# A decoder trunk on one core: the down projections take the high and the low part of an activation chunk in one product of 512 columns

## The chip, the core and the metric

The kernel runs on one core of a Trainium2 chip. The core has a matrix engine (TensorE, "PE", whose weight loads the profile lists apart as "PEld"), a vector engine (VectorE, "DVE"), a scalar engine (ScalarE, "ACT"), a general engine (GpSimd, "POOL") and a queue that issues transfers (SyncE, "SP"). Each works through its own list of instructions in order and waits on semaphores for the others. Matrix products read both operands from SBUF and add into PSUM, which has eight banks of 512 f32 columns on 128 partitions. The metric is the device time of one execution in microseconds.

## The reference, cut to what matters

The trunk has two layers on 256 tokens of width 1024. Each layer is a feed-forward block, a token mixer, and another feed-forward block, so four feed-forward blocks in all. The change touches only the last product of `swiglu`, the down projection:

```
D_MODEL = 1024
SEQ = 256
DEPTH = 2
D_FF = 256 * ((8 * D_MODEL // 3 + 255) // 256)      # 2816
...
def swiglu(x, w_in, w_out):
    gate, up = jnp.split(x @ w_in, 2, axis=-1)
    return (jax.nn.silu(gate) * up) @ w_out
...
    for i in range(DEPTH):
        x = x + 0.5 * swiglu(rms_norm(x, ffn1_norm_g[i]), ffn1_w_in[i], ffn1_w_out[i])
        hn = rms_norm(x, mix_norm_g[i])
        ...
        x = x + jnp.concatenate([y_tok, y_mem], axis=-1) @ w_out
        x = x + 0.5 * swiglu(rms_norm(x, ffn2_norm_g[i]), ffn2_w_in[i], ffn2_w_out[i])
```

## The kernel before

Activations are kept transposed: features on the 128 partitions, the 256 tokens along the columns (T = 256). To keep f32 accuracy with the faster f32r products, every operand is split into a high part (the value rounded to f32r) and a low part (the remainder). A product of a weight chunk w and an activation chunk x is then three products that add into the same 256 columns: `mm3` (L224 to L228) issues wh times xh (L225), wh times xl (L226) and wl times xh (L227). The weight chunk, 128x128, is the operand that is loaded; the activation chunk, 128x256, is streamed. Each of the three has its own load, also where the first two load the same wh.

Weights come in tiles of four chunks by 256 columns: `wtile` (L216) issues a transfer of 512 KB on SP into one of five raw buffers, ACT rounds it to wh (L211), DVE subtracts to get wl (L212), each into one of eight buffers.

A feed-forward block (`ffn`, L509) first runs `ffn_in` (L471): eleven groups, each of two banks, with gate and up halves of 256 columns; `hidden` (L473) evacuates a group: two DVE products with the norm's row (L476), a Silu on ACT, two DVE products (L479), then the split into hi and lo units of 128x512 (`split_plain`, L244 to L246: L245 a cast on ACT, L246 a subtraction on DVE). A unit of 128x512 holds two chunks of 256 tokens side by side, so hi and lo of a pair of chunks are two tiles. The 11 pairs make 22 chunks.

Then the down projection: for each pair of output blocks c2 (four of them, 256 output features each), six weight tiles are taken in turn (`KG`: five of four chunks, one of two), and for each tile both output blocks m = 0, 1 get their chunks from `products`. Both blocks lie in one bank, m = 0 in columns 0 to 255 and m = 1 in 256 to 511. When all 22 chunks are in, DVE multiplies the bank by half the norm's row (L544) and adds the residual (L546); `Norm.put` then splits the result for the next stage with the gain (ACT L132, DVE L241), squares it (ACT) and adds up the squares (DVE L288), and folds the two halves after the fourth pair (L291). The next norm's sum over features is a product with a column of ones (`chain`, line 231 of the helper `mmf`), issued by PE some 7.5 us of planned time after the block ends; between lie products of the next stage, which need the parts xh and xl but not the norm. The last pair of the last block is apart: it takes the whole weight row at once and runs m = 0 to its end before m = 1.

The order on PE and SP is the order of the program, woven by `Weave`, which counts planned PE time in `wv.now` (`mm3` counts 0.328 us). The order on ACT and DVE is chosen by the scheduler of the language.

Of the kernel before, what the change touches and what calls it, by code (L numbers as in the profile page):

```python
# [11 lines left out]
F32R = mybir.dt.float32r  # L12
# [3 lines left out]
ALU = mybir.AluOpType  # L16
# [4 lines left out]
T = 256  # L21
# [77 lines left out]
def tile_trunk(ctx: ExitStack, tc: tile.TileContext, a, out):  # L99
    nc = tc.nc  # L100
    seq = [0]

    def mk(pool, shape, dt, tag):
        seq[0] += 1
        return pool.tile(shape, dt, tag=tag, name=f"{tag}_{seq[0]}")
# [5 lines left out]
    wv = Weave()  # L111
# [16 lines left out]
    tt = nc.vector.tensor_tensor  # L128
    tabled = [None]

    def act(*args, **kw):
        ins = nc.scalar.activation(*args, **kw)  # L132
        if args[2] not in (AF.Copy, AF.Square):
            tabled[0] = ins
# [6 lines left out]
    def unit(dt):  # L141
        return mk(up, [P, 2, T], dt, "u")

    def tmp():
        return mk(tp, [P, 2, T], F32, "t")
# [4 lines left out]
    def mo():  # L150
        return mk(pb8, [P, 512], F32, "bank")

    def halves(ps):
        return ps.rearrange("p (h t) -> p h t", h=2)
# [61 lines left out]
    def wtile(src, nk, ncol=256):  # L216
        raw = mk(wrp, [P, nk, ncol], F32, "wr")
        nc.sync.dma_start(raw, src)
        return split(raw, [P, nk, ncol])

    def wcols(w, c0, kh):
        return wtile(w.rearrange("(k p) f -> p k f", p=P)[:, kh * 4:(kh + 1) * 4, c0:c0 + 256], 4)

    def mm3(ps, wh, wl, xh, xl, start, stop):  # L224
        nc.tensor.matmul(ps, wh, xh, start=start, stop=False, skip_group_check=True)  # L225
        nc.tensor.matmul(ps, wh, xl, start=False, stop=False, skip_group_check=True)  # L226
        nc.tensor.matmul(ps, wl, xh, start=False, stop=stop, skip_group_check=True)  # L227
        wv.now += 0.328  # L228
# [15 lines left out]
    def split_plain(src, hi, lo):  # L244
        nc.scalar.copy(hi, src)  # L245
        tt(out=lo, in0=src, in1=hi.bitcast(F32), op=ALU.subtract)  # L246
# [10 lines left out]
    def pair(x):  # L257
        return x.unsqueeze(1).to_broadcast([P, 2, T])
# [209 lines left out]

    KG = [(0, 4), (4, 4), (8, 4), (12, 4), (16, 4), (20, 2)]

    def ffn_in(x, w_in, hh, hl, mid=None):  # L471

        def hidden(ps):  # L473
            t = tmp()
            for m in range(2):
                tt(out=t[:, m], in0=ps[m][:, :T], in1=x.rb, op=ALU.mult)  # L476
            act(t, t, AF.Silu)
            for m in range(2):
                tt(out=t[:, m], in0=t[:, m], in1=ps[m][:, T:], op=ALU.mult)  # L479
            hi, lo = unit(F32R), unit(F32R)  # L480
            split_plain(t, hi, lo)
            hh.append(hi)
            hl.append(lo)

        waiting = []
        for gi in range(11):
            ps = [mo(), mo()]
            for kh in range(2):
                for part in range(2):
                    wh, wl = wcols(w_in, part * FF + gi * 256, kh)  # L490
                    for m in range(2):
                        for k in range(4):
                            kc = kh * 4 + k
                            mm3(ps[m][:, part * T:(part + 1) * T],
                                wh[:, k, m * P:(m + 1) * P], wl[:, k, m * P:(m + 1) * P],
                                x.xh[kc // 2][:, kc % 2], x.xl[kc // 2][:, kc % 2],
                                start=kc == 0 and part == 0, stop=kc == 7)
                        yield
            waiting.append(ps)
            if gi == 0 and not x.done:  # L500
                continue
            yield x.ready
            for ps in waiting:
                hidden(ps)
            waiting.clear()
            if mid is not None and gi == 5:
                wv.spawn(mid())

    def ffn(x, w_in, w_out, nxt=None, mid=None):  # L509

        pieces[0] = 1
        hh, hl = [], []
        yield from ffn_in(x, w_in, hh, hl, mid)
        w = w_out.rearrange("(k p) f -> p k f", p=P)

        def products(ps, m, kg, wt, start):
            ms = slice(m * P, (m + 1) * P)
            for k in range(kg[1]):
                kc = kg[0] + k
                mm3(ps, wt[0][:, k, ms], wt[1][:, k, ms], hh[kc // 2][:, kc % 2], hl[kc // 2][:, kc % 2],  # L520
                    start=kc == 0 and start, stop=kc == 21)

        for c2 in range(4):
            wts = [(kg, w[:, kg[0]:kg[0] + kg[1], c2 * 256:(c2 + 1) * 256]) for kg in KG]
            if nxt is None and c2 == 3:
                wts = [(kg, wtile(src, kg[1])) for kg, src in wts]
                y = tmp()
                for m in range(2):
                    ps = mo()[:, :T]
                    for kg, wt in wts:  # L530
                        products(ps, m, kg, wt, True)
                        yield
                    tt(out=y[:, m], in0=ps, in1=x.hrb, op=ALU.mult)
                    tt(out=y[:, m], in0=y[:, m], in1=x.xT[c2][:, m], op=ALU.add)
                    nc.scalar.dma_start(out[:, 2 * c2 + m], y[:, m])
                return
            ps = mo()
            for kg, src in wts:
                wt = wtile(src, kg[1])
                for m in range(2):  # L540
                    products(ps[:, m * T:(m + 1) * T], m, kg, wt, m == 0)
                    yield
            t = tmp()
            tt(out=t, in0=halves(ps), in1=pair(x.hrb), op=ALU.mult)  # L544
            xn = unit(F32)
            tt(out=xn, in0=t, in1=x.xT[c2], op=ALU.add)  # L546
            if nxt is None:
                nc.scalar.dma_start(out[:, 2 * c2:2 * c2 + 2], xn)
            else:
                nxt.put(xn)  # L550
        wv.spawn(nxt.chain(), LAT['norm'])
# [424 lines left out]
    def program():  # L976
        yield from memory()
        x1, x2, x3 = Norm(G_MIX, half=False), Norm(G_F2), Norm(G_F1 + 8)
        x4, x5 = Norm(G_MIX + 8, rows=False), Norm(G_F2 + 8)
        yield from ffn(x0, a["ffn1_w_in"][0], a["ffn1_w_out"][0], x1, late_constants)  # L980
        yield from mixer_a(x1, x2)
        yield from ffn(x2, a["ffn2_w_in"][0], a["ffn2_w_out"][0], x3)
        yield from ffn(x3, a["ffn1_w_in"][1], a["ffn1_w_out"][1], x4, rope_tables)
        yield from mixer_b(x4, x5)
        yield from ffn(x5, a["ffn2_w_in"][1], a["ffn2_w_out"][1])
# [41 lines left out]
```

## Time and profile before

| | |
|---|---|
| median of 3 runs | 1012.15 us (1011.66 to 1013.83) |
| the profiled execution's own time | 1012.23 us |
| its span, first to last instruction | 1010.4 us |
| granted TensorE clock, mean over the span | 1.00 |
| PE, PEld, DVE, ACT busy | 998.5, 980.2, 655.5, 519.5 us |

The profile is taken by the hardware on one execution. Its views used below are the page (busy time, the chain of work that ended last, groups of instructions by line), the timeline (start and duration of instructions, us), the chain by time, and windows (busy time of PE, PEld, DVE, ACT and POOL in a stretch, with the number of instructions, the granted clock, the share of transfers and GB/s). Products overlap in PE's pipeline, so a product's duration is longer than the distance from one start to the next; that distance is called the pitch here. In a row such as "bank<-u,wh 128*128 128x256 f32 x896" the loaded operand's shape comes first, then the streamed one's, and the count. f32r operands are printed as f32.

### The profile page before, as it was taken

The numbers are of one execution on the slowest core, as the hardware profiler recorded it, in microseconds if no ns is written. First come the engines' busy times: TensorE is split into PE (matmuls) and PEld (weight loads), VectorE is DVE, ScalarE is ACT, GpSimd is POOL, SyncE is SP. The second block draws the span as 40 slices with busy tenths as digits, with TensorE's granted clock in tenths as the row PEclk, the third lists the DMA queues.
The fourth block names the chain that finished last, engine by engine and source line by source line (L and its number), as shares of the span: only waits on it lengthen the run. The fifth ranks groups of instructions, "written<-read, shape, count | busy, mean of one in ns | idle before, by whom it ended". The sixth has DMA issues, their size and how long they took to land.

```text
span 1010.4 us, 20624 instructions
## 1 busy us (share of the span) xinstructions
PE 998.5 (99%) x8594; PEld 980.2 (97%) x8594; DVE 655.5 (65%) x1063; ACT 519.5 (51%) x764; POOL 35.7 (4%) x32
## 2 busy tenths in 40 slices
PE   8999999999999999999999999999999999999998
PEld 7999999999999999999999999999987899999998
DVE  6866665577856676665558666656787766666551
ACT  7754445446656554444445544544557754454440
POOL 1200000000001000000000000000121000000000
PEclk9999999999999999999999999999999999999999
DMA  9776656666644566665676666567541347666550
GB/s 308 242 245 200 192 180 185 199 183 179 184 139 133 167 210 195 200 189 170 192 206 205 189 191 201 173 197 198 182 131 66 100 131 220 198 189 185 188 170 21
DMA packets 173204, 182.70 MB, mean 181 GB/s; under 512 B 7124, under 2 KB 168328, under 8 KB 173112
## 3 DMA queue, kind: packets, MB, share of 16 engines
q1 hardware_dynamic: 171872, 179.60, 58.3%
q10 hardware_dynamic: 1016, 1.58, 0.5%
q8 instruction: 67, 1.10, 0.5%
q0 software_dynamic: 224, 0.22, 0.2%
q14 instruction: 25, 0.20, 0.1%
HBM read 180.32 MB, written 1.05 MB: 180 GB/s over the span
## 4 chain that ended last, share of the span: by engine, by line
PE 94%; DVE 3%; ACT 1%; DMA 1%; POOL 0%; issue 0%; SPq 0%; ACTq 0%
PE bank L225 30%; PE bank L226 30%; PE bank L227 30%; PE bank L231 2%; PE bank L236 1%; ACT u L132 1%; DVE wl L212 1%; DMA wr<-in_mem_w_kv_dram 1%; PE bank L961 1%; POOL col L379 0%; DVE col L930 0%; DVE u L383 0%; DVE col L591 0%; PE bank L925 0%; DVE u L946 0%
## 5 line engine op out<-in xcount | busy, mean ns | idle before, releaser
L212 DVE TENSOR_TENSOR wl<-wr,wh 128x1024 fp32r<-128x1024 f32 (+1 forms) x347 | 414.7, 1196 | 279.8 <-ACT wh L211 279.0
L211 ACT CAST wh<-wr 128x1024 fp32r<-128x1024 f32 (+1 forms) x347 | 356.8, 1031 | 393.1 <-PE bank L226 368.9
L225 PE MATMUL bank<-xh,wh 128*128 128x256 f32 x1544 | 429.1, 278 | 0.0
L226 PE MATMUL bank<-xl,wh 128*128 128x256 f32 x1544 | 426.8, 276 | 0.0
L227 PE MATMUL bank<-xh,wl 128*128 128x256 f32 x1544 | 426.8, 276 | 0.0
L226 PEld LDWEIGHTS bank<-xl,wh 128*128 128x128 f32 x1544 | 290.3, 188 | 0.1
L225 PEld LDWEIGHTS bank<-xh,wh 128*128 128x128 f32 x1544 | 290.0, 188 | 0.1
L227 PEld LDWEIGHTS bank<-xh,wl 128*128 128x128 f32 x1544 | 289.9, 188 | 0.0
L225 PE MATMUL bank<-u,wh 128*128 128x256 f32 x896 | 249.3, 278 | 0.0
L226 PE MATMUL bank<-u,wh 128*128 128x256 f32 x896 | 247.6, 276 | 0.0
L227 PE MATMUL bank<-u,wl 128*128 128x256 f32 x896 | 247.6, 276 | 0.0
L225 PEld LDWEIGHTS bank<-u,wh 128*128 128x128 f32 x896 | 168.2, 188 | 1.9 <-issue 1.7
L226 PEld LDWEIGHTS bank<-u,wh 128*128 128x128 f32 x896 | 168.4, 188 | 0.1
L227 PEld LDWEIGHTS bank<-u,wl 128*128 128x128 f32 x896 | 168.3, 188 | 0.0
L225 PE MATMUL bank<-wh,xh 128*128 128x256 f32 x208 | 59.7, 287 | 0.0
L226 PE MATMUL bank<-wl,xh 128*128 128x256 f32 x208 | 57.9, 278 | 0.0
L227 PE MATMUL bank<-wh,xl 128*128 128x256 f32 x208 | 57.9, 278 | 0.0
L476 DVE TENSOR_TENSOR t<-bank,rb 128x256 f32<-128x256 f32 x88 | 36.6, 420 | 7.3 <-PE bank L227 7.3
L225 PEld LDWEIGHTS bank<-wh,xh 128*128 128x128 f32 x208 | 39.1, 188 | 0.5 <-issue 0.3
L226 PEld LDWEIGHTS bank<-wl,xh 128*128 128x128 f32 x208 | 39.1, 188 | 0.1
L227 PEld LDWEIGHTS bank<-wh,xl 128*128 128x128 f32 x208 | 39.0, 187 | 0.0
L479 DVE TENSOR_TENSOR t<-t,bank 128x256 f32<-128x256 f32 x88 | 32.7, 412 | 1.8 <-ACT t L132 1.8
(171 smaller groups left out, 657.5 us busy)
## 6 DMA issues: line engine op xcount, KB each, us to landing
wr<-in_ffn_w_in_dram SPq DMA_DIRECT2D x176, 512.0 KB, 3.6
wr<-in_ffn_w_out_dram SPq DMA_DIRECT2D x80, 512.0 KB, 3.5
wr<-in_a_w_in_dram SPq DMA_DIRECT2D x28, 512.0 KB, 3.9
wr<-in_b_w_in_dram SPq DMA_DIRECT2D x14, 512.0 KB, 4.6
wr<-in_a_w_out_dram SPq DMA_DIRECT2D x12, 512.0 KB, 3.3
wr<-in_b_w_out_dram SPq DMA_DIRECT2D x12, 512.0 KB, 3.4
wr<-in_ffn_w_out_dram SPq DMA_DIRECT2D x16, 256.0 KB, 2.8
wr<-in_mem_w_kv_dram SPq DMA_DIRECT2D x7, 512.0 KB, 8.0
```

The source lines that it names most:

```text
L132: ins = nc.scalar.activation(*args, **kw)
L211: last[0] = nc.scalar.copy(hi[:, i * n:(i + 1) * n], src[:, i * n:(i + 1) * n])
L212: tt(out=lo[:, i * n:(i + 1) * n], in0=src[:, i * n:(i + 1) * n], in1=hi[:, i * n:(i + 1) * n].bitcast(F32), op=ALU.subtract)
L225: nc.tensor.matmul(ps, wh, xh, start=start, stop=False, skip_group_check=True)
L226: nc.tensor.matmul(ps, wh, xl, start=False, stop=False, skip_group_check=True)
L227: nc.tensor.matmul(ps, wl, xh, start=False, stop=stop, skip_group_check=True)
L231: nc.tensor.matmul(ps, lhsT, rhs, start=start, stop=stop, skip_group_check=True)
L236: nc.tensor.transpose(ps, src, ident[:k, :k])
L476: tt(out=t[:, m], in0=ps[m][:, :T], in1=x.rb, op=ALU.mult)
L479: tt(out=t[:, m], in0=t[:, m], in1=ps[m][:, T:], op=ALU.mult)
L961: nc.tensor.matmul(o[es[e], cs], vr[:, i, js], pTs[e][:, src], start=i == 0, stop=i == 1, skip_group_check=True)
```

## The change

Each hidden chunk gets a unit of its own with its high part in columns 0 to 255 and its low part in columns 256 to 511. In the pairs on the wide path, one product of wh takes both parts, 512 columns into a bank of its own per output block; then wl times the high part adds into the first 256 columns of it. The second half of the bank holds wh times the low part, so before the multiplication by half the norm's row ACT copies that half to SBUF and DVE adds it to the first half, for each of the two blocks. Each output pair takes two banks instead of one. The last pair of the last feed-forward block keeps the three products. In `hidden`, the split is done per chunk, 256 columns at a time.

```
--- before.py
+++ after.py
@@ -468,7 +468,7 @@
 
     KG = [(0, 4), (4, 4), (8, 4), (12, 4), (16, 4), (20, 2)]
 
-    def ffn_in(x, w_in, hh, hl, mid=None):
+    def ffn_in(x, w_in, hid, mid=None):
 
         def hidden(ps):
             t = tmp()
@@ -477,10 +477,10 @@
             act(t, t, AF.Silu)
             for m in range(2):
                 tt(out=t[:, m], in0=t[:, m], in1=ps[m][:, T:], op=ALU.mult)
-            hi, lo = unit(F32R), unit(F32R)
-            split_plain(t, hi, lo)
-            hh.append(hi)
-            hl.append(lo)
+            for m in range(2):
+                u = unit(F32R)
+                split_plain(t[:, m], u[:, 0], u[:, 1])
+                hid.append(u)
 
         waiting = []
         for gi in range(11):
@@ -509,16 +509,23 @@
     def ffn(x, w_in, w_out, nxt=None, mid=None):
 
         pieces[0] = 1
-        hh, hl = [], []
-        yield from ffn_in(x, w_in, hh, hl, mid)
+        hid = []
+        yield from ffn_in(x, w_in, hid, mid)
         w = w_out.rearrange("(k p) f -> p k f", p=P)
 
-        def products(ps, m, kg, wt, start):
+        def products(ps, m, kg, wt, wide):
+
             ms = slice(m * P, (m + 1) * P)
             for k in range(kg[1]):
                 kc = kg[0] + k
-                mm3(ps, wt[0][:, k, ms], wt[1][:, k, ms], hh[kc // 2][:, kc % 2], hl[kc // 2][:, kc % 2],
-                    start=kc == 0 and start, stop=kc == 21)
+                if wide:
+                    u = hid[kc].rearrange("p a b -> p (a b)")
+                    nc.tensor.matmul(ps, wt[0][:, k, ms], u, start=kc == 0, stop=False, skip_group_check=True)
+                    nc.tensor.matmul(ps[:, :T], wt[1][:, k, ms], u[:, :T], start=False, stop=kc == 21,
+                                     skip_group_check=True)
+                    wv.now += 0.328
+                else:
+                    mm3(ps, wt[0][:, k, ms], wt[1][:, k, ms], hid[kc][:, 0], hid[kc][:, 1], kc == 0, kc == 21)
 
         for c2 in range(4):
             wts = [(kg, w[:, kg[0]:kg[0] + kg[1], c2 * 256:(c2 + 1) * 256]) for kg in KG]
@@ -528,20 +535,23 @@
                 for m in range(2):
                     ps = mo()[:, :T]
                     for kg, wt in wts:
-                        products(ps, m, kg, wt, True)
+                        products(ps, m, kg, wt, False)
                         yield
                     tt(out=y[:, m], in0=ps, in1=x.hrb, op=ALU.mult)
                     tt(out=y[:, m], in0=y[:, m], in1=x.xT[c2][:, m], op=ALU.add)
                     nc.scalar.dma_start(out[:, 2 * c2 + m], y[:, m])
                 return
-            ps = mo()
+            ps = [mo(), mo()]
             for kg, src in wts:
                 wt = wtile(src, kg[1])
                 for m in range(2):
-                    products(ps[:, m * T:(m + 1) * T], m, kg, wt, m == 0)
+                    products(ps[m], m, kg, wt, True)
                     yield
-            t = tmp()
-            tt(out=t, in0=halves(ps), in1=pair(x.hrb), op=ALU.mult)
+            t, low = tmp(), tmp()
+            for m in range(2):
+                nc.scalar.copy(low[:, m], ps[m][:, T:])
+                tt(out=t[:, m], in0=ps[m][:, :T], in1=low[:, m], op=ALU.add)
+            tt(out=t, in0=t, in1=pair(x.hrb), op=ALU.mult)
             xn = unit(F32)
             tt(out=xn, in0=t, in1=x.xT[c2], op=ALU.add)
             if nxt is None:
```

## The prediction

> **What bounds the kernel now.** I read the page's head and its chain first, then the waits of TensorE, then stretches of the four down projections.
>
> ```profile
> span 1010.4 us, 20624 instructions
> PE 998.5 (99%) x8594; PEld 980.2 (97%) x8594; DVE 655.5 (65%) x1063; ACT 519.5 (51%) x764; POOL 35.7 (4%) x32
> PE 94%; DVE 3%; ACT 1%; DMA 1%; POOL 0%; issue 0%; SPq 0%; ACTq 0%
> ```
>
> TensorE (PE) carries 94% of the chain that ended last, and its weight loads (PEld) are nearly as busy as its products. That it is busy does not say what limits one product, so I looked at a down projection instruction by instruction. The first two fences below are the timeline at the start and at the end of the first one (start us, duration us).
>
> ```profile
> 155.81 0.28 PE L225 MATMUL bank<-u,wh 128*128 128x256 f32 x1
> 155.81 0.19 PEld L226 LDWEIGHTS bank<-u,wh 128*128 128x128 f32 x1
> 155.92 0.28 PE L226 MATMUL bank<-u,wh 128*128 128x256 f32 x1
> 155.92 0.19 PEld L227 LDWEIGHTS bank<-u,wl 128*128 128x128 f32 x1
> ...
> 215.53 0.28 PE L227 MATMUL bank<-u,wl 128*128 128x256 f32 x1
> 215.65 0.28 PE L225 MATMUL bank<-xh,wh 128*128 128x256 f32 x1
> ```
>
> From the first product of the phase (155.81) to the first of the next stage (215.65) are 59.84 us. In them lie 4 output pairs x 2 blocks x 22 chunks x 3 = 528 products, so one starts every 59.84/528 = 0.1133 us, and three (one call of `mm3`) take 0.340 us. The durations of 0.28 us overlap; it is the pitch that counts. The second thing to see is that each load starts together with the product before it, never earlier: the load for the product at 155.92 starts at 155.81.
>
> So the pitch is either the 256 columns streaming or the 128-column load. The products with a single column tell which, since they have next to nothing to stream (ones column, at the end of a norm):
>
> ```profile
> 223.70 0.30 PEld L231 LDWEIGHTS bank<-ones,acc 128*128 128x128 f32 x2
> 223.92 0.30 PEld L231 LDWEIGHTS bank<-ones,acc 128*128 128x128 f32 x2
> 224.14 0.19 PEld L225 LDWEIGHTS bank<-xh,wh 128*128 128x128 f32 x1
> ```
>
> Four loads from 223.70 to 224.14: 0.110 us each, with no stream to wait for. A load alone thus costs almost the whole 0.1133. And a long stream hides it:
>
> ```profile
> 6.37 0.38 PE L406 MATMUL bank<-t 128*128 128x512 bf16 x1
> 7.01 0.38 PE L406 MATMUL bank<-t 128*128 128x512 bf16 x1
> 299.75 0.38 PE L231 MATMUL bank<-v,u 128*128 128x257 f32 x1
> 300.84 0.38 PE L231 MATMUL bank<-v,u 128*128 128x257 f32 x1
> 299.91 1.30 PE bank L231 x6
> ```
>
> The 512-column products of the start-up run three pitches from 6.37 to 7.01, 0.213 us each (two decimals). The 257-column f32 products, which load the same 128x128 f32 block as ours, run six in 1.30 us (the last row is of the chain): 0.217 each, a load hidden in every one. I take 0.216 for a 512-column product; then 256 columns need about 0.108 for their stream, under the 0.1133 found. The down projections are bound by the weight loads, by a small margin over the stream.
>
> **The change part by part.** It acts on the wide path: 15 output pairs (four in each of three feed-forward blocks, three in the last) x 2 x 22 = 660 calls of three products.
>
> *Products.* Each call loses one load and one instruction; columns stay 768. Before: 0.340. After: the wide product takes 0.216, with the next load (0.110) hidden under it; the narrow one hides the load of the next wide one under 256 columns, as every product does now, so 0.1133. Sum 0.3293, a gain of 0.0107 x 660 = 7.1 us. The trace has no 512-column product of this type, so both ends: at the upper, every load hides and 256 columns cost half of 0.216: 0.324, gain 0.016 x 660 = 10.6. At the lower, the present cost goes with columns, 0.2267 + 0.1133 = 0.340, gain 0. And there is a slower pitch in other stages:
>
> ```profile
> 224.37 0.28 PE L226 MATMUL bank<-xl,wh 128*128 128x256 f32 x1
> 224.72 0.28 PE L226 MATMUL bank<-xl,wh 128*128 128x256 f32 x1
> ```
>
> Three products in 0.35: 0.117 each, same shapes, right after the single-column ones. If the narrow product fell into that rhythm, a call would be 0.216 + 0.117 = 0.333, gain 0.007 x 660 = 4.6. I take 7.1, because the two rows that it is made of (a hidden load of the same size, the load-bound 256) are the nearest.
>
> The Trainium skill ("TensorE: Matmul & The Clock Gate", section "Back-to-back issue gap") puts an isolated product at N/2.4 + 2.5 ns, by which 256 columns cost 109.2 and the change would save only the 2.5 of each removed product, 1.65 us in all. The rows disagree by 4 ns per product (0.1133), which I put down to the load; the same page's section on LDWEIGHTS gives columns/1.2, 106.7 ns for 128, close to the 0.110 above.
>
> *Evacuation.* Per output pair the change adds two copies on ScalarE (ACT) and two additions on VectorE (DVE), each of 128x256 from a bank, ahead of L544 and L546, which stay. *Splitting the hidden units* per half replaces one cast and one subtraction of 512 by two of 256, 44 times.
>
> ```profile
> L476 DVE TENSOR_TENSOR t<-bank,rb 128x256 f32<-128x256 f32 x88 | 36.6, 420 | 7.3 <-PE bank L227 7.3
> L246 DVE TENSOR_TENSOR u<-t,u 128x512 fp32r<-128x512 f32 x44 | 30.0, 683 | 0.0
> L245 ACT CAST u<-t 128x512 fp32r<-128x512 f32 x44 | 27.0, 613 | 0.2 <-DVE t L479 0.2
> L246 DVE TENSOR_TENSOR u<-bank,u 128x256 fp32r<-128x256 f32 x16 | 6.7, 417 | 2.8 <-ACT u L245 2.8
> L245 ACT CAST u<-bank 128x256 fp32r<-128x256 f32 x16 | 6.1, 382 | 7.0 <-PE bank L961 3.9 <-PE bank L231 3.0
> L544 DVE TENSOR_TENSOR t<-bank,hrb 128x512 f32<-128x512 f32 x15 | 10.2, 683 | 2.8 <-PE bank L227 2.8
> ```
>
> DVE gains 2 x 0.420 x 15 + (2 x 0.417 - 0.683) x 44 = 12.6 + 6.6 = 19.2 us; ACT 2 x 0.382 x 15 + (2 x 0.382 - 0.613) x 44 = 11.5 + 6.6 = 18.1 us. Inside a stage that is hidden:
>
> ```profile
> 156.00:215.00 59.00, 59.00 (x523) 59.00 (x522) 35.18 (x41) 29.75 (x36) 0.00 (x0) 1.00 0.65 184
> 365.00:470.00 105.00, 105.00 (x929) 105.00 (x928) 67.42 (x90) 50.67 (x61) 0.00 (x0) 1.00 0.63 193
> 526.28 1.05 ACT L211 CAST wh<-wr 128x1024 fp32r<-128x1024 f32 x1 [1.67 <-PE bank L226]
> 529.00 1.05 ACT L211 CAST wh<-wr 128x1024 fp32r<-128x1024 f32 x1 [1.67 <-PE bank L226]
> ```
>
> In a down stretch (first row; after PE and PEld come DVE, ACT) DVE works 35 of 59 us and would work 38; in an input stretch 67 of 105. The casts wait for PE to give back one of eight weight buffers, so they run about seven tiles of 2.72 us ahead: a copy that makes ACT wait for PE for 1 or 2 us delays nothing. The extra bank per output pair (8 in turn) and the 22 hidden units (as many as before) come round in the old distance. The copy that reads columns 256 to 511 waits for the wide products and blocks ACT's queue behind it, where only casts with that lead stand.
>
> *The three edges* where a down projection ends and the next stage begins are where cover is short. There the last pair's evacuation, the gain split, the squares and the fold (L291) must be done before PE comes to the ones product (L231):
>
> ```profile
> 215.50 1.23 DVE L212 TENSOR_TENSOR wl<-wr,wh 128x1024 fp32r<-128x1024 f32 x1 [1.49 <-ACT wh L211]
> 216.64 0.68 DVE L544 TENSOR_TENSOR t<-bank,hrb 128x512 f32<-128x512 f32 x1
> 217.24 1.22 DVE L212 TENSOR_TENSOR wl<-wr,wh 128x1024 fp32r<-128x1024 f32 x1
> 218.38 0.68 DVE L546 TENSOR_TENSOR u<-t,u 128x512 f32<-128x512 f32 x1
> 222.40 0.36 DVE L291 TENSOR_TENSOR acc<-acc 128x256 f32<-128x256 f32 x1
> 536.83 0.43 DVE L291 TENSOR_TENSOR acc<-acc 128x256 f32<-128x256 f32 x1
> 538.28 0.30 PEld L231 LDWEIGHTS bank<-ones,acc 128*128 128x128 f32 x2
> 717.58 0.43 DVE L291 TENSOR_TENSOR acc<-acc 128x256 f32<-128x256 f32 x1
> 718.92 0.30 PEld L231 LDWEIGHTS bank<-ones,acc 128*128 128x128 f32 x2
> 217.30:223.70 6.40, 6.40 (x59) 6.40 (x59) 6.07 (x12) 2.71 (x6) 0.00 (x0) 1.00 0.65 173
> ```
>
> The fold ends 0.94, 1.02 and 0.91 us before the load that needs it (222.76 to 223.70, 537.26 to 538.28, 718.01 to 718.92). The last row shows DVE busy 6.07 of 6.40 us there, so the two additions push the fold back by about their 0.84. The copies cost less: block 0 closes two chunks (0.66) before block 1, and DVE is held by a subtraction (L212 to 216.73) while ACT copies. Lateness 0.8 to 1.0 against 0.91 to 1.02 leaves a stall of 0 to 0.1; one more L212 (1.22) slipping in front makes it 1.2. I take 0.2 each, 0.6 in all, ends 0 and 3.6. The end of the kernel is on the old path (`mm3`) and does not move.
>
> Sum: 7.1 - 0.6 = 6.5 us off the profiled execution's 1012.2 (span 1010.4 and 1.8 around it), which stands at the median of the runs shown, 1012.15. Forecast **1005.7 us**.
>
> **The rivals.**
>
> *A fixed cost per product.* If 0.1133 is 0.108 of stream and 0.0053 that any product pays, a wide one is 0.2213, a call 0.3346, the gain 0.0054 x 660 = 3.6, the time 1012.2 - 3.6 + 0.6 = 1009.2. The slow rhythm above lands near (1008.2). For it: load and stream are too close to separate by one row. Against: 257 f32 columns pay 0.217 with nothing on top.
>
> *The smaller fixed cost.* The gap between the 0.216 and the 512 columns streamed at the rate of the 0.213 rows is about 0.003; if only that goes per removed product, 2.0 us go and 0.6 come back: 1010.8. The formula of the Trainium skill weighed above ("TensorE: Matmul & The Clock Gate", "Back-to-back issue gap") would give 1012.2 - 1.65 + 0.6 = 1011.2, an estimate. Against: the four single-column loads at 0.110.
>
> *Cost by columns* (the product disappears, its time does not): gain 0, time 1012.8. For it: no product of this type over 256 columns is in the trace. Against: both 512 and 257 columns cost less than twice 0.1133.
>
> *All loads hidden*: 0.324 a call, 10.6 - 0.6, time 1002.2. Against: a narrow product still has only 256 columns over the next load.
>
> *The edges turn it round.* ACT is a queue; should the low copies and the gain split each land behind a cast that waits for PE (one per 2.72 us), the fold is 5.4 + 0.9 late, the stall 6.3 - 0.95 = 5.4 at each of three edges, 16 in all: 1012.2 - 7.1 + 16.2 = 1021.3. It decides from a lateness over the present slack of 7.1/3 = 2.4 us. For it: DVE is nearly full there and slack is under 1.1. Against: the copies become ready before the cast's buffer does, so an order by readiness puts them first.
>
> **How the numbers follow.** Forecast 0.60 (own range 1004 to 1007.5), fixed cost or slow rhythm 0.14, all hidden 0.08, smaller fixed cost 0.04, by columns 0.07, edges 0.07. The range from 1002.0 to 1010.5 holds the first three. Faster by over 0.2% (2.0 us, about what a measurement of this kernel can tell from no change): 0.60 + 0.14 + 0.08 = 0.82. Within 0.2%: 0.04 + 0.07 = 0.11. Slower: 0.07.
>
> **What would show it.** A group of 660 products of 128x512 and 660 of 128x256 in place of the three lines; a wide start to the next start of 0.216, narrow to wide 0.113; the first down phase 176 x 0.3293 = 58.0 us instead of 59.84, the last (44 old calls) 58.4. At the edges, waits of PE's L231 for L291 under 0.3 us. A wide pitch of 0.22 to 0.227 proves a rival on the products; L231 waiting over 2.4 us proves the edges.

## The result, and the profile after

| | before | after |
|---|---|---|
| median, us | 1012.95 | 1027.74 |
| lowest to highest, us | 1011.66 to 1013.83 (4 runs) | 1026.66 to 1028.96 (4 runs) |
| profiled execution: own time / span, us | 1012.23 / 1010.4 | 1028.58 / 1026.7 |
| ratio of the times (95% interval) | | 1.0148 (1.0135 to 1.0160) |

The changed kernel is about 15 us slower; 6.5 us faster was forecast. The first fence has lines of the page of the changed kernel: the head, the busy engines, and the two groups of products that stand where three lines of 256 columns stood.

```profile
span 1026.7 us, 19409 instructions
PE 1013.8 (99%) x7934; PEld 965.0 (94%) x7934; DVE 673.7 (66%) x1137; ACT 533.0 (52%) x838; POOL 33.8 (3%) x32
...
L523 PE MATMUL bank<-u,wh 128*128 128x512 f32 x660 | 233.3, 397 | 0.0
L524 PE MATMUL bank<-u,wl 128*128 128x256 f32 x660 | 185.5, 281 | 0.0
```

There are 660 fewer products (8594 to 7934), as counted, and TensorE is as full as before (99%). So it did less and took longer over it. Its idle time can't be the reason: 12.9 us in all (1026.7 less 1013.8), against 11.9 before. The next fence is the timeline of TensorE in the changed kernel (start us, duration us): the start and the end of the first down projection, then the start and the end of the input stage of the third feed-forward block, whose code the change does not touch (`xh`, `xl` against `wh`, `wl`).

```profile
157.73 0.39 PE L523 MATMUL bank<-u,wh 128*128 128x512 f32 x1
157.95 0.28 PE L524 MATMUL bank<-u,wl 128*128 128x256 f32 x1
158.07 0.40 PE L523 MATMUL bank<-u,wh 128*128 128x512 f32 x1
158.31 0.28 PE L524 MATMUL bank<-u,wl 128*128 128x256 f32 x1
...
219.91 0.28 PE L225 MATMUL bank<-xh,wh 128*128 128x256 f32 x1
...
537.34 0.28 PE L225 MATMUL bank<-xh,wh 128*128 128x256 f32 x1
...
662.40 0.39 PE L523 MATMUL bank<-u,wh 128*128 128x512 f32 x1
```

The first wide product takes about 0.22 (157.73 to 157.95), the second 0.24 (158.07 to 158.31), and the later ones 0.235 by their starts. The phase lasts from 157.73 to 219.91, 62.18 us; in it are 4 output pairs x 2 x 22 = 176 calls, so a call takes 0.3533, where three products took 0.340 before and 0.3293 was forecast. Of it a wide product takes 0.235 and a narrow one 0.118. The third input stage lasts 125.06 us, from 537.34 to 662.40. In the kernel before, the same two marks stand at

```profile
530.23 0.28 PE L225 MATMUL bank<-xh,wh 128*128 128x256 f32 x1
...
651.03 0.28 PE L225 MATMUL bank<-u,wh 128*128 128x256 f32 x1
```

120.80 us apart. That untouched stage lost 4.26 us, almost twice what a changed phase lost (2.34). Two windows show both facts by count. The columns are the window, its length, busy time and instructions of PE, PEld, DVE, ACT and POOL, the granted clock, the DMA share and GB/s. Before, first a down projection and then the third input stage:

```profile
160.00:210.00 50.00, 50.00 (x444) 50.00 (x443) 30.30 (x35) 24.11 (x30) 0.00 (x0) 1.00 0.69 198
560.00:620.00 60.00, 60.00 (x532) 60.00 (x531) 38.01 (x50) 28.87 (x33) 0.00 (x0) 1.00 0.64 195
```

After, the same two windows:

```profile
160.00:210.00 50.00, 50.00 (x285) 43.42 (x284) 31.24 (x42) 25.81 (x37) 0.00 (x0) 1.00 0.64 186
560.00:620.00 60.00, 60.00 (x512) 60.00 (x511) 38.04 (x56) 28.45 (x38) 0.00 (x0) 1.00 0.60 189
```

In 50 us of a down projection there were 444 products, 148 calls; now there are 285, some 142 calls. The weight loads now leave 6.58 of 50 us free (43.42 busy) and the calls are still longer, so loads are not what limits them. In 60 us of the third input stage 532 products became 512 at the same granted clock (1.00) with no more DMA: 60.28/532 = 0.1133 and 60.28/512 = 0.1177 each (0.28 more than the window, because the products at its edges count whole). I call these the quick and the slow rhythm. The kernel before is quick in its feed-forward blocks and slow for a moment after a norm.

Where the 16.3 us of span went, from start to start in the two timelines: four down phases 2.34 each, 9.3; the third input stage 4.3; the mixers 0.5 and 0.3; the start-up 1.9 (the first down projection starts at 157.73 instead of 155.81). The second and fourth input stages did not change (120.80). The start-up is not the change's: a later kernel below with the same code up to there (the one with one more broadcast) starts its first down projection at 155.86. The other 14.4 are its price.

### The profile page after: what moved, and what is told of

Its sections match the earlier page's. It is cut to its first block, busy times and chain, and to the rows that moved or that the text cites. A ratio compares the mean times of both kernels' runs of the same rounds, so it can differ in the third digit from the quotient of the medians.

```text
span 1026.7 us, 19409 instructions
## 1 busy us (share of the span) xinstructions
PE 1013.8 (99%) x7934; PEld 965.0 (94%) x7934; DVE 673.7 (66%) x1137; ACT 533.0 (52%) x838; POOL 33.8 (3%) x32
## 4 chain that ended last, share of the span: by engine, by line
PE 94%; DVE 3%; ACT 1%; DMA 1%; POOL 0%; issue 0%; SPq 0%; ACTq 0%
PE bank L225 22%; PE bank L226 22%; PE bank L227 22%; PE bank L523 15%; PE bank L524 8%; PE bank L231 2%; PE bank L236 1%; ACT u L132 1%; DVE wl L212 1%; DMA wr<-in_mem_w_kv_dram 1%; PE bank L971 1%; POOL col L379 0%; DVE col L940 0%; DVE u L383 0%; DVE col L601 0%
## 5 line engine op out<-in xcount | busy, mean ns | idle before, releaser
L523 PE MATMUL bank<-u,wh 128*128 128x512 f32 x660 | 233.3, 397 | 0.0
L524 PE MATMUL bank<-u,wl 128*128 128x256 f32 x660 | 185.5, 281 | 0.0
L523 PEld LDWEIGHTS bank<-u,wh 128*128 128x128 f32 x660 | 124.1, 188 | 30.4
L225 PE MATMUL bank<-u,wh 128*128 128x256 f32 x236 | 67.3, 285 | 0.0
L226 PE MATMUL bank<-u,wh 128*128 128x256 f32 x236 | 65.6, 278 | 0.0
L227 PE MATMUL bank<-u,wl 128*128 128x256 f32 x236 | 65.6, 278 | 0.0
L245 ACT CAST u<-t 128x256 fp32r<-128x256 f32 x88 | 35.0, 403 | 40.5 <-DVE t L479 40.5
L225 PEld LDWEIGHTS bank<-u,wh 128*128 128x128 f32 x236 | 44.5, 189 | 1.9 <-issue 1.7
L226 PEld LDWEIGHTS bank<-u,wh 128*128 128x128 f32 x236 | 44.5, 188 | 0.1
```

What stands on the lines that cost most here:

```text
L523: nc.tensor.matmul(ps, wt[0][:, k, ms], u, start=kc == 0, stop=False, skip_group_check=True)
L524: nc.tensor.matmul(ps[:, :T], wt[1][:, k, ms], u[:, :T], start=False, stop=kc == 21, skip_group_check=True)
```

## The experiments

### Two probes: products alone, and under traffic

The trace of before had no 512-column product of the kernel's reduced f32 type (`fp32r`). The first probe has runs of such products of 128x128 weights over four banks, without other work; the second has weight transfers, casts and subtractions beside them, as in the kernel. They compute nothing of the reference, and each ran once.

```
mm(banks[i % 4][:, :n], w(i), m(i, n))        # n = 256, 512, 128, 192, 320, 384
mm(banks[i % 4], w(i), m(i, 512)); mm(banks[i % 4][:, :256], w(i + 1), m(i, 256))
```

> A probe of products alone, no other engine at work; it computes nothing of the reference (its output is x). Runs of equal products with a 128x128 load each: f32r of 256 and 512 columns, 512 and 256 in turn, then 128, 192, 320, 384 columns, and bf16 of 512 and 256. Theory 'columns' (an f32r stream costs 0.443 ns a column at best, 0.460 in a slow rhythm, whatever the load, and the load of 0.110 is a floor only under that): 512 alone 0.227 to 0.235, a pair 512 + 256 0.340 to 0.354, 384 at 0.170 to 0.177, 320 at 0.142 to 0.147, 128 and 192 at 0.110 to 0.114, bf16 of 512 0.216. Theory 'load-bound' (the prediction's): 512 alone 0.216, 384 at 0.163, 320 at 0.136, and the 235 of the changed kernel then comes from the other engines' or the transfers' traffic.

The timeline of the first probe: a row is a stretch of a run of products, from its first start to its last end, with the shape of the first one (the third row has both sizes in turn). The pitch is the row's time, less one product's own duration, over the count less one.

```profile
19.80 5.44 PE L57 MATMUL bank<-mv,wgt 128*128 128x256 f32 x44
25.66 6.52 PE L57 MATMUL bank<-mv,wgt 128*128 128x512 f32 x28
38.58 7.82 PE L57 MATMUL bank<-mv,wgt 128*128 128x512 f32 x43
71.24 4.96 PE L57 MATMUL bank<-mv,wgt 128*128 128x128 f32 x43
81.94 6.32 PE L57 MATMUL bank<-mv,wgt 128*128 128x320 f32 x42
89.00 8.31 PE L57 MATMUL bank<-mv,wgt 128*128 128x384 f32 x47
97.81 9.01 PE L57 MATMUL bank<-xb,wb 128*128 128x512 bf16 x41
107.74 4.42 PE L57 MATMUL bank<-xb,wb 128*128 128x256 bf16 x39
```

| columns | pitch, us | columns x 0.000417 | left over |
|---|---|---|---|
| 256 | (5.44 - 0.28)/43 = 0.1200 | 0.1067 | 0.0133 |
| 320 | (6.32 - 0.30)/41 = 0.147 | 0.1333 | 0.013 |
| 384 | (8.31 - 0.34)/46 = 0.173 | 0.160 | 0.013 |
| 512 | (6.52 - 0.39)/27 = 0.227 | 0.2133 | 0.014 |
| 512 and 256 in turn (third row, 21 pairs) | (7.82 - 0.40)/21 = 0.353 | 0.320 | 0.033 for two |
| bf16 512 | (9.01 - 0.38)/40 = 0.2158 | 0.2133 | 0.0025 |
| bf16 256 | (4.42 - 0.27)/38 = 0.1092 | 0.1067 | 0.0025 |

The rate of 0.000417 us a column is the slope of both types (f32: 0.227 - 0.120 over 256 columns). The 128-column row stands at 0.112 ((4.96 - 0.27)/42): there the load does set the pace. From 256 columns up it does not. Neither theory holds in full. Were it the loads, 512 would have cost 0.216 and 320 columns 0.136. The ranges of the theory of columns held from 320 to 512, but by columns alone 512 would cost twice the 0.1200 of 256, 0.240, and it costs 0.227. Each f32 product pays its columns and a fixed part: 13.3 ns here, where the kernel before pays 0.1133 - 0.1067 = 6.7, and its slow rhythm 11.1. A bf16 product pays 2.5. The Trainium skill ("TensorE: Matmul & The Clock Gate", "Back-to-back issue gap") has N/2.4 + 2.5 ns for an isolated product, 109.2 and 215.8 for these two sizes; the bf16 rows agree (0.1092 and 0.2158), the f32 rows do not (0.1200 and 0.227).

The pair in turn took 0.353 by itself, the same as the call of the changed kernel. Here the mixture is dearer than its parts: 0.227 + 0.120 = 0.347. The third probe, below, has pairs that are not.

> The same probe while transfers of 512 KB, ACT casts and DVE subtractions of 128x1024 run beside it as in a down projection. Theory 'columns': the same pitches as in the probe alone within 2%. Theory 'traffic': 256 alone goes from under 0.113 to 0.118 or 512 alone from 0.216 to 0.235 with the traffic on.

The second probe: a run of 512 columns with traffic, and its window.

```profile
25.73 5.61 PE L57 MATMUL bank<-mv,wgt 128*128 128x512 f32 x24
26.00:31.00 5.00, 5.00 (x24) 4.14 (x23) 3.58 (x3) 2.87 (x3) 0.00 (x0) 1.00 0.92 304
```

(5.61 - 0.39)/23 = 0.227 again, with the DMA engines at 0.92 and VectorE and ScalarE at work. The whole block of 224 products of 256, of 512 and of both in turn lasts 33.38 us in either probe. Traffic has no part in it.

### The change with the wide product cut in two

Everything of the change stays (layout of the hidden units, two banks, evacuation in two steps); only the 512 columns are two products again.

```diff
-                    nc.tensor.matmul(ps, wt[0][:, k, ms], u, start=kc == 0, stop=False, skip_group_check=True)
+                    nc.tensor.matmul(ps[:, :T], wt[0][:, k, ms], u[:, :T], start=kc == 0, stop=False, skip_group_check=True)
+                    nc.tensor.matmul(ps[:, T:], wt[0][:, k, ms], u[:, T:], start=False, stop=False, skip_group_check=True)
```

> The changed kernel with the wide product made as two of 256 columns into the two halves of the same bank; units, banks, copies and additions stay as changed. If the wide product alone costs the time (and the slow rhythm after it), the first down phase takes 59.84 us again, the third feed-forward input 120.8, and the kernel 1012 to 1014. If the evacuation, the split per chunk or the extra banks cost it: 1020 or more. ACT and DVE at the three edges alone: 0 to 3.6 us over the kernel before.

1013.08 us (10 runs), ratio to before 1.000 (0.9982 to 1.0017). The marks of its first down projection:

```profile
155.87 0.28 PE L523 MATMUL bank<-u,wh 128*128 128x256 f32 x1
...
215.71 0.28 PE L225 MATMUL bank<-xh,wh 128*128 128x256 f32 x1
```

59.84 us, as before, and the third input stage has its 120.80 again. VectorE is busy 673.5 us and ScalarE 532.1 in this kernel, as in the changed one. Its span is 1011.0, 0.6 over the kernel before, and that 0.6 stands in the first mixer (134.53 instead of 133.94 us): at the first edge TensorE waits for the low parts of the activations (L241), which VectorE now delivers later.

```profile
222.34 0.19 PEld L226 LDWEIGHTS bank<-xl,wh 128*128 128x128 f32 x1 [0.44 <-DVE xl L241]
222.35 0.39 PE L226 MATMUL bank<-xl,wh 128*128 128x256 f32 x1 [0.24 <-DVE xl L241]
```

So layout, extra bank, copies, additions and edges cost 0.6 us by the spans, too little to tell in the times of the runs. All the rest of the loss comes from the 512-column product, what it hands on included.

### Wide products together, then narrow ones

Per tile and output chunk all wide products come first, then all narrow ones, so that sizes change twice in eight products.

```diff
             for k in range(kg[1]):
...
+                nc.tensor.matmul(ps, wt[0][:, k, ms], u, start=kc == 0, stop=False, skip_group_check=True)
+            for k in range(kg[1]):
...
+                nc.tensor.matmul(ps[:, :T], wt[1][:, k, ms], hid[kc][:, 0], start=False, stop=kc == 21,
+                                 skip_group_check=True)
```

> The changed kernel with, for each weight tile and block, its four wide products first and then its four narrow ones, instead of in turn. If it is the switching between 512 and 256 that throws PE into the slow rhythm, calls go back to 0.340 (phase 59.8 to 60.5, kernel 1013 to 1016). If any 512-column product does it: 62.2 and 1026 to 1029 as changed.

1017.25 us (10 runs), ratio 1.0039 (1.0018 to 1.0060), between the two times that were expected; its timeline:

```profile
179.65 1.09 PE L527 MATMUL bank<-u,wh 128*128 128x512 f32 x4
180.57 0.62 PE L530 MATMUL bank<-u,wl 128*128 128x256 f32 x4
...
182.42 0.85 PE L527 MATMUL bank<-u,wh 128*128 128x512 f32 x3
```

Eight calls from 179.65 to 182.42, 0.346 each; a phase takes 61.01. This order gives back about 10 of the 15 us: half of the extra cost of a call (0.3533 to 0.3467, against 0.340), and the third input stage, which lasts 120.8. It still loses to three products of 256. As many loads and columns in another order cost another time, which neither a load nor a stream as the bound can explain.

### What the fixed part hangs on

A third probe runs products of 256 and of 512 in one bank or several, with the same or changing weights and streams, in the kernel's triples, and with loads of 64 columns. It computes nothing of the reference.

> A second probe of products alone, its output x: what sets the fixed part of an f32r product over N/2.4 ns, which was 6.7 ns in the kernel before (256 columns), 13.3 in the first probe (256 to 512 columns, a new bank, new weights and a new stream each time) and 16.7 in its 512-256 turns. Runs with one of these changed at a time, eight bf16 products between them. If the change of bank costs it: 256 columns in one bank at 0.1133, banks in turn at 0.120. If a shared stream or shared weights between neighbours save it: the runs with the same x or the same w at 0.1133, the others at 0.120. If the load costs it: a load of 64 columns brings 256 to 0.109 and 512 to 0.216. The kernel's own triples: 0.340 for three by all. 512 and 256 in one bank as in the changed kernel: 0.353 a pair.

```profile
25.78 5.44 PE L62 MATMUL bank<-xh,wh 128*128 128x256 f32 x44
...
70.72 6.53 PE L62 MATMUL bank<-xh,wh 128*128 128x512 f32 x28
...
88.89 0.28 PE L62 MATMUL bank<-xh,wl 128*128 128x256 f32 x1
...
95.82 0.28 PE L62 MATMUL bank<-xh,wl 128*128 128x256 f32 x1
...
128.81 5.39 PE L62 MATMUL bank<-xh,wh 128*64 128x256 f32 x46
...
136.69 6.15 PE L62 MATMUL bank<-xh,wh 128*64 128x512 f32 x26
```

One bank gives 0.1200 and 0.227, as four banks in turn did. The same stream, the same weights, and the kernel's own triples gave 0.1200 too, although the very same triples take 0.1133 in the kernel. So operands and banks do not set the rhythm here.

The pairs of 512 and 256 in one bank, with the operands of the changed kernel, missed what was expected of them: twenty pairs from 88.89 to 95.82 take 0.347 each, not 0.353, and three variants of them (the same weights, the other half of the stream, a second bank) take 0.347 as well. That is just the sum of the parts, 0.227 + 0.120. So taking the two sizes in turn is not enough to make a call cost 0.3533, and that the first probe gave the kernel's number does not explain the kernel. No run separates in what the two probes differ here (banks in turn, the order of the weights, what ran before).

Loads of half the size (half the output rows, too) give 0.1136 for 256 columns and (6.15 - 0.39)/25 = 0.230 for 512. At 512 columns the load is not the bound: half of it makes the product no cheaper. At 256 it took 6 ns off the 0.1200, but 0.109 was expected if the load cost the fixed part. What sets the fixed part stays open; this probe found no setting that gives 512 columns in under 0.227.

### Wide products in one block only

Wide products stay in the second feed-forward block; the others have two halves.

```diff
+                    if one:
                         nc.tensor.matmul(ps, wt[0][:, k, ms], u, start=kc == 0, stop=False, skip_group_check=True)
+                    else:
+                        nc.tensor.matmul(ps[:, :T], wt[0][:, k, ms], u[:, :T], start=kc == 0, stop=False, skip_group_check=True)
+                        nc.tensor.matmul(ps[:, T:], wt[0][:, k, ms], u[:, T:], start=False, stop=False, skip_group_check=True)
...
-        yield from ffn(x2, a["ffn2_w_in"][0], a["ffn2_w_out"][0], x3)
+        yield from ffn(x2, a["ffn2_w_in"][0], a["ffn2_w_out"][0], x3, one=True)
```

> The changed kernel with wide products in the second feed-forward block alone, and two halves of 256 in the other three. If the wide products cost 13.2 ns a call there and nothing else: that down phase 62.2 instead of 59.84, the kernel 2.3 us over the kernel with halves everywhere. If the slow rhythm is handed on as in the changed kernel: also 125 instead of 120.8 for the third block's input, 6.6 over in all.

1022.98 us (4 runs), ratio 1.0099 (1.0082 to 1.0116); the span, 1020.1, is 9.1 above that of the two halves (1011.0). Three stretches of it: the first down projection (two halves), the third input stage, the third down projection (two halves).

```profile
160.00:210.00 50.00, 50.00 (x444) 50.00 (x442) 32.30 (x42) 25.74 (x37) 0.00 (x0) 1.00 0.67 198
560.00:620.00 60.00, 60.00 (x512) 60.00 (x511) 37.28 (x53) 28.66 (x38) 0.00 (x0) 1.00 0.60 186
660.00:710.00 50.00, 50.00 (x427) 50.00 (x426) 31.25 (x41) 25.83 (x37) 0.00 (x0) 1.00 0.60 182
```

Ahead of the wide block the same code runs 444 products in 50 us, behind it 427. From start to start, the wide phase itself lost 2.34, the third input stage 4.26 and the third down projection, which has no wide product, 2.35. That is 8.95 of the 9.1; 6.6 had been expected, without the third down projection. Wide products cost more behind them than where they stand.

The slow rhythm is not one unbroken stretch. The norm of the third block has two short groups of full-precision products, the single-column ones and a broadcast. Between them 45 products run quick (542.30 to 547.20), and behind the broadcast it is slow again. The changed kernel does the same. With two halves it is the other way round: quick, slow between the two groups, then quick.

```profile
542.30:547.20 4.90, 4.90 (x45) 4.90 (x44) 4.18 (x17) 1.58 (x3) 0.70 (x1) 1.00 0.70 211
```

### A group of full-precision products behind the wide ones

In the changed kernel the second block is followed at once by the third; the others are followed by a mixer. One more broadcast of a norm (products of full f32, whose result nothing uses) goes ahead of the third block, first in the changed kernel, then in the one with two halves.

```diff
         yield from ffn(x2, a["ffn2_w_in"][0], a["ffn2_w_out"][0], x3)
+        bcast_rows(mo(), x2.rc)
         yield from ffn(x3, a["ffn1_w_in"][1], a["ffn1_w_out"][1], x4, rope_tables)
```

> The changed kernel with one norm broadcast more (four f32 products of 128 columns into a bank that nobody reads, 0.44 us) between the second block's down projection and the third block's input. In the traces so far each such group, and each group of single-column products, seems to turn PE's rhythm over between 0.1133 and 0.1178. If so, the third input takes 120.8 to 121.3 instead of 125.06, and the kernel comes 3 to 4.5 us under the changed one. If the slow input has another cause (buffers, ACT, DVE): 125 stays and the kernel is 0.4 over the changed one.

1023.5 us (4 runs), ratio 1.0105 (1.0088 to 1.0122), 4.2 under the median of the changed kernel (1027.74). The third input stage:

```profile
560.00:620.00 60.00, 60.00 (x532) 60.00 (x531) 39.33 (x56) 30.22 (x41) 0.00 (x0) 1.00 0.63 193
```

532 products, the quick rhythm again, and 121.56 us from start to start instead of 125.06, the group's own 0.4 included: 3.5 of the 4.2; the rest lies within the spread of the changed kernel's runs. So the group changes which rhythm the stage ends up in. It does not break the slow one at once. Ahead of the norm's groups it goes on,

```profile
537.00:544.00 7.00, 7.00 (x62) 7.00 (x61) 6.69 (x10) 3.43 (x5) 0.00 (x0) 1.00 0.74 219
```

7.28/62 = 0.1174 each, and the quick one begins behind the block's own broadcast (550.51).

> The same extra broadcast at the same place in the kernel with two halves, whose third input takes 120.8. If the group turns the rhythm over, that input now becomes slow, 125, the down projection after it 62.2 instead of 59.84, and the kernel 6 to 7.5 us slower than without (1019 to 1021), with no 512-column product in it. If it only ever mends: 1013.5.

1013.51 us (10 runs), ratio 1.0005 (0.9991 to 1.0020). I had expected that every such group turns the rhythm over, so that a quick stage behind it becomes slow. Stretches of the third input stage, near its start and later:

```profile
532.00:538.00 6.00, 6.00 (x53) 6.00 (x53) 5.76 (x9) 3.47 (x6) 0.00 (x0) 1.00 0.65 200
560.00:620.00 60.00, 60.00 (x532) 60.00 (x531) 38.55 (x54) 29.08 (x38) 0.00 (x0) 1.00 0.64 194
```

A moment of the slow rhythm behind the group (118 products in two runs, by their starts), and then the quick one. That theory fell. Behind the extra group the two kernels take the same course, 118 slow products and then quick ones, 121.56 us in both, although one came to it slow and the other quick. So here the group sets the rhythm anew, and I can't say beforehand which one comes. In the first probe such a group changes nothing. The run of 256 columns behind it,

```profile
52.47 0.61 PE L92 MATMUL bank<-wraw 128*128 128x128 f32 x4
52.83 6.00 PE L57 MATMUL bank<-mv,wgt 128*128 128x256 f32 x48
```

takes (6.00 - 0.28)/47 = 0.1217 a product, the first one 0.20 and the others 0.120 as ahead of the group.

### The low product in bf16

If a bf16 product pays 2.5 ns and an f32 one 6.7 or more, one of the three in bf16 might win. The kernel before with the product of the low weights in bf16 (low weights and a copy of the high hidden units rounded to it, one raw weight buffer fewer):

```diff
+                nc.tensor.matmul(ps, wt[1][:, k, ms], hb, start=False, stop=kc == 21, skip_group_check=True)
```

> The kernel before with the third product of the down projections (low part of the weights times high part of the activations) in bf16: DVE writes the low weights as bf16 at no extra instruction, ACT makes a bf16 copy of each hidden unit, four raw buffers instead of five for the space. The first probe has bf16 of 256 columns at 0.1092. If the f32r products keep their 0.1133 beside it: 0.3358 a call, 704 calls, 2.9 us under the kernel before (1009.3). If the change of type throws the rhythm to 0.1178 or 0.120: 0.345 to 0.349, 3.4 to 6.5 us over it in these phases, and more in what follows.

1029.47 us (4 runs), ratio 1.0165 (1.0150 to 1.0180). Its timeline:

```profile
179.79 0.37 PE L529 MATMUL bank<-u,wh 128*128 128x256 f32 x1
179.99 0.28 PE L530 MATMUL bank<-u,wh 128*128 128x256 f32 x1
180.11 0.28 PE L532 MATMUL bank<-hb,wl 128*128 128x256 bf16 x1
180.15 0.36 PE L529 MATMUL bank<-u,wh 128*128 128x256 f32 x1
```

A call takes 0.36 by these rows and 64.05/176 = 0.364 over the phase, where 0.3358 was expected. TensorE waits for nothing in that phase, so neither the copies nor the missing buffer hold it up. The f32 product behind a bf16 one starts 0.04 after it, but the next start comes 0.20 later; changing the type twice a call costs 24 ns over the three products at 0.340, more than the bf16 product can save.

### The wide product alone

The narrow product is left out in the wide path, and with it the low weights' part of those sums.

```diff
-                    nc.tensor.matmul(ps[:, :T], wt[1][:, k, ms], u[:, :T], start=False, stop=kc == 21,
-                                     skip_group_check=True)
```

> The changed kernel with the narrow products left out (the weights' low part is not used in the wide path), so 512-column products only, coming from a stage in the fast rhythm. If a 512-column product costs its columns and 13.3 ns as in the probe alone: 0.2268 a product, 176 of them 39.9 us for the first down phase. If what it costs in the changed kernel is its own: 0.235, 41.3 us. At 0.216, the prediction's price: 38.0 us.

951.71 us (one run). Six wide products in a row:

```profile
179.72 1.56 PE L523 MATMUL bank<-u,wh 128*128 128x512 f32 x6
```

(1.56 - 0.40)/5 = 0.232, and 41.06/176 = 0.2333 over the phase, with only one load per 512 columns. In the kernel a wide product is dear without its narrow partner, too: 0.233, not the 0.227 of the probes. Subtracting it from the call leaves 0.12 for the narrow one.

No version that computes the whole sum was faster than the kernel before. The lowest steady pitch of a 512-column product in any run is 0.227, twice the quick 256 (0.1133); with a quick narrow product that is 0.340, what the three products cost already.

## Why the prediction was wrong

**What failed** is the step "The down projections are bound by the weight loads, by a small margin over the stream", and with it the term "the wide product takes 0.216". It measured 0.235, above every rival's price and above the 0.22 to 0.227 by which a rival was to be known. The load of 128 columns does take 0.11 and does end last at 128 columns (0.112 in the first probe). From 256 columns up the probe shows stream plus a fixed part of the product. By the same slope the kernel's quick pitch is 0.1067 + 0.0067 = 0.1133, which happens to lie near the load; that a product of 256 columns with half the load still took 0.1136 speaks for this reading, though no run shows it in the kernel itself. For the wide product the step is refuted: it hid its load and cost 0.235 all the same. The prediction had one size of this type, and from one size these two readings can't be told apart. It said so in the rival, and gave that 0.14.

**The rows that priced it** were of other types. The 512-column rows are bf16, which pays 2.5 ns. The 257-column rows print as f32, but they are full-precision products: in the first probe two such instructions give four records (52.47 above), and a record of 257 columns takes 0.217, 0.84 ns a column, twice the 0.417 of the kernel's type. So 0.217 was the pitch of a slower kind of product and not the price of twice 256 columns with "a load hidden in every one". That two unlike rows gave the same number looked like a confirmation and was chance.

**The narrow product** was put at 0.1133 and measured 0.118. The prediction had seen the slow rhythm (0.117 after a norm) and priced it for the narrow product alone, 4.6 in place of 7.1; it did not ask what sets that rhythm or whether a stage keeps it. It holds over most of a stage and goes on into code that was not changed: 4.3 us in the third input stage.

**The bounds.** "Lower end gain 0" took the quick rhythm for both products, 0.2267 + 0.1133. The measured call loses 13.3 ns, 660 x 0.0133 = 8.8 us where a gain of 7.1 was forecast, a term wrong by 15.9; the handed-on part and the mixers (5.1) had no term at all. No row excluded a loss there; the range should have held one.

**The rivals.** The fixed cost per product was right in kind, but took the cost for a constant, 5.3 ns, that each removed product gives back. A 256-column product pays 6.7 in the quick rhythm; a product in the alternating pair pays (0.3533 - 0.320)/2 = 16.7. For the price of the products, cost by columns came nearest (0.2267 and 0.1133 against 0.235 and 0.118). The edges had the nearest time (1021.3 against 1027.74) and the right direction, by luck: the loss came from the products themselves.

**What was right.** VectorE gained 18.2 us (673.7 - 655.5; 19.2 forecast) and ScalarE 13.5 (18.1 forecast), hidden but for the 0.6 of the kernel with two halves. That 0.6 equals what the prediction put in for the three edges, by luck: it stands at the first edge alone, and TensorE waits there for L241, which the prediction did not price, and not for L291. Folds and the loads that need them in the changed kernel, first and last edge:

```profile
227.54 0.41 DVE L291 TENSOR_TENSOR acc<-acc 128x256 f32<-128x256 f32 x1
228.46 0.52 PEld L231 LDWEIGHTS bank<-ones,acc 128*128 128x128 f32 x4
...
731.41 0.42 DVE L291 TENSOR_TENSOR acc<-acc 128x256 f32<-128x256 f32 x1
732.94 0.53 PEld L231 LDWEIGHTS bank<-ones,acc 128*128 128x128 f32 x4
```

The fold is done 0.51 us early at the first (227.95 to 228.46) and 1.11 at the last, and no wait of TensorE for L291 appears. Counted from the end of the down projection, the fold of the first edge came 0.93 later than before (227.95 - 219.91 against 222.76 - 215.65), as the forecast lateness of 0.8 to 1.0 has it; the slack fell by only 0.43, because the ones product came later, too. At the last edge the fold came only 0.12 later. The 660 calls and the unchanged count of columns were right too.

**What stays open** is what sets the fixed part. The runs show 6.7, 11.1, 13.3 and 16.7 ns for the same type, that in the kernels it depends on what ran before, and that in the probes traffic, banks and shared operands do not set it. Why 512 and 256 in turn take 0.353 in the kernel and the first probe and 0.347 in the third is open as well. No run shows the mechanism.

## What to carry to other kernels

A new shape of a product should be priced in its own data type with a short probe of two or three sizes in the order in which the kernel will run them; rows of another type that agree in shape prove nothing, and one size can't separate a load from a fixed part. Where TensorE is full, fewer and larger products are not cheaper by themselves: compare pitches per column, and look for the cheapest pitch that any steady run shows before rewriting a loop. After such a change compare the pitch of untouched stages too, since a part of the price may stand there.

## What the runs showed of the hardware

- A reduced-f32 product of 256 columns and more costs 0.417 ns a column and a fixed part that is no constant: 6.7 (quick), 11.1 (slow), 13.3 (alone in a probe, and in the third probe's pairs) and 16.7 ns (512 and 256 in turn in the changed kernel and the first probe). A bf16 product has 2.5.
- The rhythm outlasts its cause: 256-column products ran at 0.1177 instead of 0.1133 through most of the third input stage and the down projection after it, 187 us in all, behind one phase of 512-column products (in the kernel with one wide block). Some 45 products between the norm's two groups were quick.
- A short group of full-precision products put ahead can change which rhythm a stage ends up in (125.06 to 121.56 us in the third input stage); in the first probe it changed nothing.
- An f32 product right behind a bf16 one is dear: changing type twice in three products made 0.340 into 0.364.
- Nothing of this shows as waiting or as a lower clock: TensorE is 99% busy in both rhythms and the windows show a clock of 1.00 for both; only counts per window or differences of starts tell them apart.
